# Hybrid decoder layer on one core: constants in three packed arrays, their transpositions and the bias product right behind the first tile's, one cast given to VectorE

## The chip, the cores and the metric

The kernel runs on 1 core of one Trainium2 chip. The metric is the device time of one execution in microseconds (us), lower is better. Before the change it was measured in three runs.

## What is computed

One decoder layer over 512 tokens of 1024 features, all in float32. Cut to what matters here:

```python
u = rms_norm(x, norm_mix_g)
proj = u @ w_in                       # q 1024, k 256, v 256, conv value and gate 2048, two gates 2048
q = rms_norm(q, q_norm_g) * HEAD_DIM ** -0.5
k = rms_norm(k, k_norm_g)
attn = sliding_window_attention(q, k, v, attn_sinks, rel_bias) @ w_attn_o   # window 128, bias by distance bucket
h = a * sigmoid(gate)
h = depthwise_conv(h, w_dw) + b_dw    # 31 taps, 1024 channels
conv = silu(layer_norm(h, conv_ln_g, conv_ln_b)) @ w_conv_out
x = x + (sigmoid(gate_attn) * attn + sigmoid(gate_conv) * conv) @ w_out
x = x + square(relu(rms_norm(x, norm_mlp_g) @ w_ff1)) @ w_ff2
```

The constants that the change speaks of are small: `w_dw` (31 rows of 1024), `b_dw`, `conv_ln_g` and `conv_ln_b` (one row of 1024 each), `rel_bias` (32 x 16), a one-hot array of 32 x 128 that maps distances to buckets, `q_norm_g` and `k_norm_g` (64 each) and `attn_sinks` (16).

## The kernel before

Every operand of a product is split into a high part (rounded to fp32r) and a low part (the remainder), and a product is three matmuls: high by high, low by high, high by low. So weights arrive as `raw_...` tiles, ScalarE casts the high half, and GpSimd or VectorE subtracts to get the low half.

*Start.* The 512 tokens are four tiles of 128. For each tile ScalarE squares and sums (`x_square`, L296), VectorE finishes the root and scales (`x_scale`, L300, output `u`), TensorE transposes (L207, eight transpositions into `tp_u`), ScalarE casts the high part out of PSUM (`uTh`, L209) and VectorE the remainder (`uTl`, L210). The key weights `raw_k` come in two halves of 512 rows; `hi_lo` (L305) casts one half (L307) and returns the function that subtracts (L308). `k_proj` (ps_k, L316, L317 and, with the low weights, L320) and `v_proj` (ps_v, the same lines) follow for each tile. Before the first tile's transpositions TensorE runs `WARM` = 20 matmuls of the identity with itself into a PSUM tile that nobody reads, and between these transpositions and the first `k_proj` it runs `FILL` = 4 more of them (a float32 matmul is two passes, so the profile has 40 and 8).

*Constants.* All loads of this time go through SP's queue. The constants come in nine loads behind the x tiles and the k and v weights: `gq`, `gk`, the sinks, `w_dw`, `b_dw`, `conv_ln_g`, `conv_ln_b`, `rel_bias`, `oh`. The four that hold channels land in one tile `rows` of 34 partitions. `columns` (L358) transposes it on TensorE in eight pieces into `wc_ps`, multiplies `rel_bias` by the one-hot array into `rel_ps`, and on VectorE copies both out (`wcol`, `lnh`, `rel`); `rel` goes to DRAM, from where the attention bias is read back. `columns` is the first of the events that follow the k and v projections.

*Order.* The start is written out by hand (the block under `manual_schedule`, from L1367) for TensorE, VectorE, ScalarE and GpSimd; each engine takes its instructions in that order. After the last `v_proj` the list `events` is sorted by position and called: at -2 the constants, at 0 the first tile of the convolution's gate (`ps_g`, L498 to L500), at 0.4 `k_norm`, at 4.5 the cast of the normed keys (`k2h`, L397), at 9.5 their transposition (`ktp_h`, L405).

*SP's loads.* A load counts up one of eight completion counters, which are taken in turn. SP issues in order, and a load that takes a counter again waits until the load before it on that counter has landed in full. So the ninth load on SP waits for the landing of the first, the tenth for that of the second, and so on, if nothing else holds it longer. Before, the order is: x tile 0, gmix, raw_k (two halves), x tile 1, raw_v (two halves), x tiles 2 and 3, and the nine constants. A later load of weights also waits until its buffer (`raw`, two buffers) is free.

Of the kernel before, what the change touches and what calls it, by code (L numbers as in the profile page):

```python
# [17 lines left out]
P = 128  # L18
# [21 lines left out]
RATES = ((16, 1.0), (42, 1.9), (152, 1.35), (1e9, 1.8))  # L40
WARM = 20
FILL = 4
EARLY = 3
# [10 lines left out]
def tile_hybrid_block(  # L54
# [4 lines left out]
    w_in: bass.AP,  # L59
    q_norm_g: bass.AP,  # L60
    k_norm_g: bass.AP,
    attn_sinks: bass.AP,
    rel_bias: bass.AP,
    w_attn_o: bass.AP,
    w_dw: bass.AP,
    b_dw: bass.AP,
    conv_ln_g: bass.AP,
    conv_ln_b: bass.AP,
    w_conv_out: bass.AP,
# [3 lines left out]
    w_ff2: bass.AP,  # L73
    onehot: bass.AP,
    out: bass.AP,
# [150 lines left out]

    warm_up(WARM)

    def load_x(t):
# [19 lines left out]

    rows = att.tile([P, D], F32, name="rows", tag="qraw", bufs=2)  # L250
    rb_sink = whole_lines(keep, P, LINE // 4, "rb_sink")
    rb = rb_sink[0:32, 16:16 + NQ]
    oh = sm.tile([32, P], F32, name="oh", tag="osb", bufs=1)
    gq = keep.tile([P, HD], F32, name="gq")
    gk = keep.tile([P, HD], F32, name="gk")
    nsink = rb_sink[:, 32:32 + NQ]
    nc.sync.dma_start(gq, bc(q_norm_g[0], P))
    nc.sync.dma_start(gk, bc(k_norm_g[0], P))
    nc.sync.dma_start(nsink, bc(attn_sinks[0], P))
    nc.sync.dma_start(rows[0:CW, :], w_dw[0])  # L260
    nc.sync.dma_start(rows[CW:CW + 1, :], b_dw)
    nc.sync.dma_start(rows[CW + 1:CW + 2, :], conv_ln_g)
    nc.sync.dma_start(rows[CW + 2:CW + 3, :], conv_ln_b)
    nc.sync.dma_start(rb, rel_bias)
    nc.sync.dma_start(oh, onehot)

# [90 lines left out]

    def columns():  # L358
        wc_ps = ps1.tile([P, KD, NR], F32, name="wc_ps", tag="s")
        for k in range(KD):  # L360
            pe.transpose(wc_ps[:, k, :], rows[0:NR, k * P:(k + 1) * P], ident[0:NR, 0:NR])
        rel_ps = ps1.tile([P, P], F32, name="rel_ps", tag="s")
        pe.matmul(rel_ps[0:NQ, :], rb, oh, start=True, stop=True)
        ve.memset(rel, NEG)
        ve.tensor_copy(wcol, wc_ps)
        ve.tensor_scalar(out=wcol[:, :, 0:CW], in0=wc_ps[:, :, 0:CW], scalar1=0.5, scalar2=None, op0=ALU.mult)
        ve.tensor_scalar(out=lnh, in0=wc_ps[:, :, CW + 1:CW + 3], scalar1=0.5, scalar2=None, op0=ALU.mult)
        ve.tensor_copy(rel[:, P:2 * P], rel_ps[0:NQ, :])
        nc.sync.dma_start(rel_d, rel)

    def rep(ap, n):
# [36 lines left out]

    at(-2, columns)
    at(0.4, k_norm)  # L410
# [955 lines left out]

    with tc.manual_schedule(engines=START_ENGINES):  # L1367
        se.activation(roots[:, 0:1], epsc, AF.Sqrt)
        x_square(0, ss0)
        x_scale(0, rsqrt_root(root[0], mean_eps(ss0, D, 1, "x0"), 1, "x0"))  # L1370
        lo0 = hi_lo(kw, kw_raw, 0, se.copy, ge)
        lo0()
        load(0)
        x_trans(0)
        warm_up(FILL)
        lo1 = hi_lo(kw, kw_raw, 1, se.copy, ve)
        lo1()
# [36 lines left out]
        ksum()
        for _ in vp:
            pass
        k_proj(3)()
        for _ in v_proj(3):
            pass
        for _, _, fn, args in sorted(events, key=lambda e: e[:2]):  # L1420
            fn(*args)


_INS = ["x", "norm_mix_g", "w_in", "q_norm_g", "k_norm_g", "attn_sinks", "rel_bias", "w_attn_o", "w_dw", "b_dw",
        "conv_ln_g", "conv_ln_b", "w_conv_out", "w_out", "norm_mlp_g", "w_ff1", "w_ff2"]
_OUT = (S, D)
# [33 lines left out]
```

## Time and profile before

| what | value |
|---|---|
| median of 3 runs | 758.69 us (757.81 to 758.85) |
| the profiled execution's own time | 757.91 us |
| its span, first to last instruction | 756.1 us |
| granted TensorE clock, mean | 0.999 |
| TensorE (PE) busy | 750.6 us, 99% |
| VectorE (DVE) busy | 606.0 us, 80% |
| ScalarE (ACT) busy | 441.3 us, 58% |
| GpSimd (POOL) busy | 273.4 us, 36% |

Times in the profile are microseconds from the first instruction. PE is TensorE's matmuls, PEld its weight loads, SPq the issue of a load by SP. "out<-in" names the tile written and the tiles read, L and a number is a line of the kernel before. A bracket at a row's end says how long the engine had been idle and what ended it. The chain is followed back from the last instruction to what released it. A windows row gives a stretch, its length, the busy time of each engine with the number of starts in parentheses, the granted clock (1.00 is full), the share of the 16 DMA engines and GB/s. A DMA row gives 40 equal slices of its stretch.

### The profile page before, as it was taken

The page shows a single profiled execution, that of the slowest core. Times are in us where ns is not written, and L with a number is a line of the kernel's source. Part 1 is how long each engine was busy: PE and PEld are TensorE (multiplying, and loading weights), DVE is VectorE, ACT ScalarE, POOL GpSimd, SP SyncE. Part 2 cuts the span into 40 slices and gives each one's busy share as a digit, 9 for nine tenths or more (in the row PEclk, how much of TensorE's full clock was granted, in tenths as well). Part 3 has the DMA queues.
Part 4 walks back from the last instruction along what each step waited for, and adds up shares of the span by engine and source line. Part 5 has one row for each costly group of instructions (what it writes and reads, how often), then busy time and mean ns, then how long its engine had stood idle before and what let it go on. Part 6 is the DMA issues. An engine that isn't in the chain of part 4 may idle for free.

```text
span 756.1 us, 11678 instructions
## 1 busy us (share of the span) xinstructions
PE 750.6 (99%) x4474; PEld 663.6 (88%) x4474; DVE 606.0 (80%) x928; ACT 441.3 (58%) x697; POOL 273.4 (36%) x214
## 2 busy tenths in 40 slices
PE   9999999999999999999999999999999999999997
PEld 8989989898888888888888899988998899889986
DVE  5466998789878988878346679899879987998795
ACT  7445457757666665339235357864676467636861
POOL 1453968948774566443531002210121012101210
PEclk9999999999999999999999999999999999999999
DMA  7441040312314113531338205983498349834772
GB/s 262 149 161 56 1 168 15 126 56 81 115 61 137 56 55 112 168 111 56 112 111 294 97 29 91 263 198 117 127 230 200 112 123 228 203 116 115 171 162 111
DMA packets 66014, 97.48 MB, mean 129 GB/s; under 512 B 3540, under 2 KB 36612, under 8 KB 65958
## 3 DMA queue, kind: packets, MB, share of 16 engines
q1 hardware_dynamic: 56710, 78.91, 31.2%
q0 software_dynamic: 9248, 17.83, 13.4%
q8 instruction: 35, 0.57, 0.3%
q14 instruction: 21, 0.17, 0.1%
HBM read 94.60 MB, written 2.12 MB: 128 GB/s over the span
## 4 chain that ended last, share of the span: by engine, by line
PE 98%; DVE 2%; issue 0%; POOL 0%; DVEq 0%; POOLq 0%
PE ps_x L1177 12%; PE ps_z L1182 12%; PE ps_y L1182 6%; PE ps_y L1177 6%; PE ps_z L1177 3%; PE ps_x L1182 3%; PE ps_g L498 2%; PE ps_q L197 2%; PE ps_q L198 2%; PE ps_q L199 2%; PE ps_a L498 2%; PE ps_ta L498 2%; PE ps_a L500 2%; PE ps_g L500 2%; PE ps_g L499 2%; PE ps_ta L500 2%
## 5 line engine op out<-in xcount | busy, mean ns | idle before, releaser
L1148 DVE TENSOR_TENSOR piecel<-block,pieceh 128x1024 fp32r<-128x1024 f32 x112 | 135.7, 1219 | 27.8 <-ACT pieceh L1145 27.6
L1145 ACT CAST pieceh<-block 128x1024 fp32r<-128x1024 f32 x112 | 116.7, 1050 | 67.5 <-DVE block L1138 21.7
L803 DVE SCALAR_TENSOR_TENSOR cv<-h,wcol,cv 128x512 f32<-128x512 f32 x208 | 146.2, 746 | 0.5
L1124 POOL DMA_DIRECT2D block<-in_w_ff_dram x34 | 41.3, 1241 | 287.3 <-DVE piecel L1148 157.1
L1177 PE MATMUL ps_x<-xSh,pieceh 128*128 128x256 f32 x192 | 53.0, 276 | 0.0
L1177 PE MATMUL ps_x<-xSl,pieceh 128*128 128x256 f32 x192 | 53.0, 276 | 0.0
L1177 PE MATMUL ps_x<-xSh,piecel 128*128 128x256 f32 x192 | 53.0, 276 | 0.0
L711 ACT ACTIVATE s<-s,negm 128x257 f32<-128x257 f32 (+1 forms) x64 | 30.4, 479 | 16.0 <-DVE negm L703 16.0
L1182 PE MATMUL ps_z<-piecel,aSh 128*128 128x512 f32 (+1 forms) x98 | 37.9, 387 | 0.0
L1182 PE MATMUL ps_z<-pieceh,aSh 128*128 128x512 f32 (+1 forms) x98 | 37.7, 385 | 0.0
L1182 PE MATMUL ps_z<-pieceh,aSl 128*128 128x512 f32 (+1 forms) x98 | 37.7, 385 | 0.0
L1138 DVE TENSOR_TENSOR block<-block,block 128x1024 f32<-128x1024 f32 x30 | 36.5, 1221 | 0.8 <-DMA block<-in_w_ff_dram 0.4
L795 POOL TENSOR_TENSOR side<-side,tap 128x512 f32<-128x512 f32 x24 | 31.2, 1298 | 15.1 <-ACT tap L794 15.1
L197 PE MATMUL ps_q<-wh_q,uTh 128*128 128x256 f32 x128 | 36.5, 285 | 0.0
L199 PE MATMUL ps_q<-wh_q,uTl 128*128 128x256 f32 x128 | 36.2, 283 | 0.0
L198 PE MATMUL ps_q<-wl_q,uTh 128*128 128x256 f32 x128 | 36.2, 283 | 0.0
L1177 PEld LDWEIGHTS ps_x<-xSh,piecel 128*128 128x128 f32 x192 | 36.0, 188 | 0.0
L1177 PEld LDWEIGHTS ps_x<-xSh,pieceh 128*128 128x128 f32 x192 | 36.0, 188 | 0.0
L1177 PEld LDWEIGHTS ps_x<-xSl,pieceh 128*128 128x128 f32 x192 | 36.0, 188 | 0.0
L735 DVE TENSOR_TENSOR pTl<-ptp,pTh 128x512 fp32r<-128x512 f32 x28 | 19.0, 686 | 17.8 <-ACT pTh L731 17.8
L720 POOL TENSOR_TENSOR s<-s,r 128x1024 f32<-128x1024 f32 (+1 forms) x16 | 26.9, 1684 | 16.7 <-DVE r L715 16.7
L1216 ACT CAST aSh<-c 128x1024 fp32r<-128x1024 f32 x16 | 16.8, 1053 | 21.4 <-DVE c L1230 11.7
(325 smaller groups left out, 2531.8 us busy)
## 6 DMA issues: line engine op xcount, KB each, us to landing
block<-in_w_ff_dram SPq DMA_DIRECT2D x64, 512.0 KB, 5.5
block<-in_w_ff_dram POOLq DMA_DIRECT2D x34, 512.0 KB, 6.9
x<-in_x_dram SPq DMA_DIRECT2D x8, 512.0 KB, 4.2
raw_g<-in_w_in_dram SPq DMA_DIRECT2D x8, 512.0 KB, 4.4
raw_a<-in_w_in_dram SPq DMA_DIRECT2D x8, 512.0 KB, 3.5
raw_q<-in_w_in_dram SPq DMA_DIRECT2D x8, 512.0 KB, 4.5
raw_ta<-in_w_in_dram SPq DMA_DIRECT2D x8, 512.0 KB, 4.3
raw_tc<-in_w_in_dram SPq DMA_DIRECT2D x8, 512.0 KB, 3.5
```

What stands on the lines that cost most here:

```text
L197: pe.matmul(ps, ah, wh, start=first, stop=False)
L198: pe.matmul(ps, ah, wl, start=False, stop=False)
L199: pe.matmul(ps, al, wh, start=False, stop=last)
L498: pe.matmul(ps, wh[:, k, :], ah(k), start=(k == 0), stop=False)
L500: pe.matmul(ps, wl[:, k, :], ah(k), start=False, stop=(k == KD - 1))
L803: ve.scalar_tensor_tensor(out=cps[ct], in0=src, scalar=w, in1=cps[ct], op0=ALU.mult, op1=ALU.add)
L1124: ge.dma_start(tl["raw"][buf][:, ks, :], block(ph, i, j)[:, ks, :], accum_op=ALU.add)
L1138: ve.tensor_tensor(out=o, in0=a, in1=b, op=ALU.add)
L1145: se.copy(piece("h", n), tl["raw"][buf][:, 2 * h:2 * h + 2, :])
L1148: ve.tensor_tensor(out=piece("l", n), in0=tl["raw"][buf][:, 2 * h:2 * h + 2, :], in1=piece("h", n).bitcast(F32), op=ALU.subtract)
L1177: pe.matmul(o, b[:, c, w], a[:, k, :], start=(first and c + q + i == 0), stop=(k == 3 and i == 2), skip_group_check=True)
L1182: pe.matmul(acc[:, cols], a[:, k, w], b[:, c, cols], start=(first and c + i == 0), stop=(k == 3 and i == 2), skip_group_check=True)
```

## The change

Three packed arrays, joined before the launch, take the place of nine: `vectors` (q_norm_g, k_norm_g, attn_sinks: 144 numbers), `buckets` (rel_bias and the one-hot array: 32 x 144) and `channels` (w_dw, b_dw, conv_ln_g, conv_ln_b: 34 x 1024). `channels` and `buckets` are loaded right behind raw_k, ahead of x tile 1; `vectors` behind x tile 3. `columns` is cut in two: `columns_in` (TensorE) takes the place of the four filler matmuls, and `columns_out` (VectorE and the write of `rel`) stays where `columns` was. Both results of `columns_in` share one PSUM bank. `WARM` is 17 instead of 20 and stands in the block that is written by hand. The high cast of raw_k's first half goes from ScalarE to VectorE.

```diff
-WARM = 20
-FILL = 4
+WARM = 17
...
-    warm_up(WARM)
...
     nc.sync.dma_start(gmix, bc(norm_mix_g[0], P))
+    rows = att.tile([P, D], F32, name="rows", tag="qraw", bufs=2)
+    bucket = sm.tile([32, NQ + P], F32, name="bucket", tag="osb", bufs=1)
+    rb, oh = bucket[:, 0:NQ], bucket[:, NQ:NQ + P]
     load_kv(kw_raw, Q_END, 0)
     load_kv(kw_raw, Q_END, 1)
+    nc.sync.dma_start(rows[0:CW + 3, :], channels)
+    nc.sync.dma_start(bucket, buckets)
     xt.append(load_x(1))
...
-    nc.sync.dma_start(gq, bc(q_norm_g[0], P))
-    nc.sync.dma_start(gk, bc(k_norm_g[0], P))
-    nc.sync.dma_start(nsink, bc(attn_sinks[0], P))
-    nc.sync.dma_start(rows[0:CW, :], w_dw[0])
-    nc.sync.dma_start(rows[CW:CW + 1, :], b_dw)
-    nc.sync.dma_start(rows[CW + 1:CW + 2, :], conv_ln_g)
-    nc.sync.dma_start(rows[CW + 2:CW + 3, :], conv_ln_b)
-    nc.sync.dma_start(rb, rel_bias)
-    nc.sync.dma_start(oh, onehot)
+    vecs = whole_lines(keep, P, 3 * LINE // 4, "vecs")
+    gq, gk, nsink = vecs[:, 0:HD], vecs[:, HD:2 * HD], vecs[:, 2 * HD:2 * HD + NQ]
+    nc.sync.dma_start(vecs[:, 0:2 * HD + NQ], bc(vectors[0], P))
...
-    def columns():
-        wc_ps = ps1.tile([P, KD, NR], F32, name="wc_ps", tag="s")
+    def columns_in():
+        bank = ps1.tile([P, S], F32, name="wc_rel", tag="s")
+        wc_ps = bank[:, 0:KD * NR].rearrange("p (k n) -> p k n", n=NR)
         for k in range(KD):
             pe.transpose(wc_ps[:, k, :], rows[0:NR, k * P:(k + 1) * P], ident[0:NR, 0:NR])
-        rel_ps = ps1.tile([P, P], F32, name="rel_ps", tag="s")
+        rel_ps = bank[:, S - P:S]
         pe.matmul(rel_ps[0:NQ, :], rb, oh, start=True, stop=True)
+        cols_ps.extend((wc_ps, rel_ps))
+
+    def columns_out():
...
+    at(-2, columns_out)
...
-    at(-2, columns)
...
     with tc.manual_schedule(engines=START_ENGINES):
+        warm_up(WARM)
...
-        lo0 = hi_lo(kw, kw_raw, 0, se.copy, ge)
+        lo0 = hi_lo(kw, kw_raw, 0, ve.tensor_copy, ge)
         lo0()
         load(0)
         x_trans(0)
-        warm_up(FILL)
+        columns_in()
```

TensorE at its start, before and after (`wc_rel` is the shared PSUM bank, `bucket` holds both operands of the bias product; the line numbers after are smaller by 7 to 17 here):

```order
L225 MATMUL warm<-ident 128x128 x20
L207 MATMUL tp_u_0_183<-ident,u_167 128x128 x4
L207 MATMUL tp_u_1_190<-ident,u_167 128x128 x4
L225 MATMUL warm<-ident 128x128 x4
L316 MATMUL ps_k_208<-kw_152,uTh 128x256
L317 MATMUL ps_k_208<-kw_152,uTl 128x256
```

```order
L218 MATMUL warm<-ident 128x128 x17
L200 MATMUL tp_u_0_172<-ident,u_156 128x128 x4
L200 MATMUL tp_u_1_179<-ident,u_156 128x128 x4
L347 MATMUL wc_rel<-ident,rows 128x34 x8
L349 MATMUL wc_rel<-bucket 16x128
L299 MATMUL ps_k_203<-kw_124,uTh 128x256
L300 MATMUL ps_k_203<-kw_124,uTl 128x256
```

The filler between the transpositions and the first `k_proj` became nine instructions that wait for two loads. Those loads, in SP's queue before and after:

```order
L231 DMA x_115<-in_x_dram 128x1024
L241 DMA gmix<-in_norm_mix_g_dram 128x1024
L235 DMA raw_k<-in_w_in_dram 128x4x256 x2
L231 DMA x_122<-in_x_dram 128x1024
L235 DMA raw_v<-in_w_in_dram 128x4x256 x2
L231 DMA x_127<-in_x_dram 128x1024
L231 DMA x_129<-in_x_dram 128x1024
L257 DMA gq<-in_q_norm_g_dram 128x64
L258 DMA gk<-in_k_norm_g_dram 128x64
L259 DMA rb_sink<-in_attn_sinks_dram 128x16
L260 DMA rows<-in_w_dw_dram 31x1024
```

```order
L222 DMA x_95<-in_x_dram 128x1024
L232 DMA gmix<-in_norm_mix_g_dram 128x1024
L226 DMA raw_k<-in_w_in_dram 128x4x256 x2
L238 DMA rows<-in_channels_dram 34x1024
L239 DMA bucket<-in_buckets_dram 32x144
L222 DMA x_106<-in_x_dram 128x1024
L226 DMA raw_v<-in_w_in_dram 128x4x256 x2
L222 DMA x_111<-in_x_dram 128x1024
L222 DMA x_113<-in_x_dram 128x1024
L248 DMA vecs<-in_vectors_dram 128x144
L441 DMA raw_g_169<-in_w_in_dram 128x4x256 x2
```

The constants' 34 rows moved from behind x tile 3 to ahead of x tile 1 and raw_v. TensorE again, at the end of the last `v_proj`, before and after:

```order
L320 MATMUL ps_v_487<-vw_155,uTh 128x256 x8
L361 MATMUL wc_ps<-ident,rows 128x34 x8
L363 MATMUL rel_ps<-oh,rb_sink 16x128
L498 MATMUL ps_g_534<-uTh,wh_g_0_364 128x512
L499 MATMUL ps_g_534<-uTl,wh_g_0_364 128x512
```

```order
L303 MATMUL ps_v_482<-vw_127,uTh 128x256 x8
L490 MATMUL ps_g_518<-uTh,wh_g_0_359 128x512
L491 MATMUL ps_g_518<-uTl,wh_g_0_359 128x512
L492 MATMUL ps_g_518<-uTh,wl_g_0_360 128x512
L490 MATMUL ps_g_518<-uTh,wh_g_0_359 128x512
```

The first gate tile now follows the v projection directly. On ScalarE the cast of raw_k's first half is gone ahead of the first `uTh`, and on VectorE it stands between `x_scale` of tile 0 and the first `uTl`; nothing else moves on these two engines.

More of the change, by code (lines that the diff above doesn't have):

```diff
@@ L59, in tile_hybrid_block @@
     w_in: bass.AP,
[L60 to L63, printed above, removed]
+    vectors: bass.AP,
+    buckets: bass.AP,
     w_attn_o: bass.AP,
[L65 to L68, printed above, removed]
+    channels: bass.AP,
     w_conv_out: bass.AP,
@@ L73, in tile_hybrid_block @@
     w_ff2: bass.AP,
-    onehot: bass.AP,
     out: bass.AP,
@@ L248, in tile_hybrid_block @@
     xt += [load_x(2), load_x(3)]
[L250 to L256, printed above, removed]
-    nc.sync.dma_start(gq, bc(q_norm_g[0], P))
-    nc.sync.dma_start(gk, bc(k_norm_g[0], P))
[L259 to L262, printed above, removed]
-    nc.sync.dma_start(rows[CW + 2:CW + 3, :], conv_ln_b)
-    nc.sync.dma_start(rb, rel_bias)
-    nc.sync.dma_start(oh, onehot)
+    vecs = whole_lines(keep, P, 3 * LINE // 4, "vecs")
+    gq, gk, nsink = vecs[:, 0:HD], vecs[:, HD:2 * HD], vecs[:, 2 * HD:2 * HD + NQ]
+    nc.sync.dma_start(vecs[:, 0:2 * HD + NQ], bc(vectors[0], P))
     uTh = keep.tile([P, KD, S], F32R, name="uTh", tag="act", bufs=2)
@@ L356, in tile_hybrid_block @@
     rel_d = dr.tile([NQ, 3 * P], F32, name="rel_d")
-    def columns():
-        wc_ps = ps1.tile([P, KD, NR], F32, name="wc_ps", tag="s")
+    cols_ps = []
+    def columns_in():
+        bank = ps1.tile([P, S], F32, name="wc_rel", tag="s")
+        wc_ps = bank[:, 0:KD * NR].rearrange("p (k n) -> p k n", n=NR)
         for k in range(KD):
             pe.transpose(wc_ps[:, k, :], rows[0:NR, k * P:(k + 1) * P], ident[0:NR, 0:NR])
-        rel_ps = ps1.tile([P, P], F32, name="rel_ps", tag="s")
+        rel_ps = bank[:, S - P:S]
         pe.matmul(rel_ps[0:NQ, :], rb, oh, start=True, stop=True)
+        cols_ps.extend((wc_ps, rel_ps))
+    def columns_out():
+        wc_ps, rel_ps = cols_ps
         ve.memset(rel, NEG)
@@ L1421, in tile_hybrid_block @@
             fn(*args)
-_INS = ["x", "norm_mix_g", "w_in", "q_norm_g", "k_norm_g", "attn_sinks", "rel_bias", "w_attn_o", "w_dw", "b_dw",
-        "conv_ln_g", "conv_ln_b", "w_conv_out", "w_out", "norm_mlp_g", "w_ff1", "w_ff2"]
+_INS = ["x", "norm_mix_g", "w_in", "vectors", "buckets", "w_attn_o", "channels", "w_conv_out", "w_out", "norm_mlp_g",
+        "w_ff1", "w_ff2"]
 _OUT = (S, D)
@@ L1449 @@
     nc = _bacc.Bacc("TRN2", target_bir_lowering=False, num_devices=1, dynamic_dma_scratch_size=2048)
+    packed = dict(inputs)
+    packed["vectors"] = _np.concatenate([inputs[n] for n in ("q_norm_g", "k_norm_g", "attn_sinks")], axis=1)
+    packed["buckets"] = _np.concatenate([inputs["rel_bias"], _bucket_onehot()], axis=1)
+    packed["channels"] = _np.concatenate([inputs["w_dw"][0]] + [inputs[n] for n in ("b_dw", "conv_ln_g", "conv_ln_b")])
     arrays, args = {}, []
-    for name in _INS + ["onehot"]:
-        a = _bucket_onehot() if name == "onehot" else _np.ascontiguousarray(inputs[name])
+    for name in _INS:
+        a = _np.ascontiguousarray(packed[name])
         arrays[f"in_{name}_dram"] = a
```

## The prediction

> **What bounds the kernel now.** I read the page first, then TensorE's waits, the chain of the first 18 us and of 34 to 40 us, then the loads of that time. From the page (busy time; the chain's shares by engine), and from the waits of TensorE:
>
> ```profile
> PE 750.6 (99%) x4474; PEld 663.6 (88%) x4474; DVE 606.0 (80%) x928; ACT 441.3 (58%) x697; POOL 273.4 (36%) x214
> ...
> PE 98%; DVE 2%; issue 0%; POOL 0%; DVEq 0%; POOLq 0%
> ...
> PE warm L225 <- POOL eps_ln L122: 1.5, 1, 1.5
> ```
>
> TensorE is the bound from start to end, and the only wait listed for it is the first 1.5 us. So a microsecond that TensorE loses or saves near the start reaches the end, and work on the other engines counts only where TensorE waits for it. The chain (start, length, what), first at the start, then at the end of the k and v projections:
>
> ```profile
> 1.47 7.24 PE warm L225 x40
> 8.71 0.87 PE tp_u L207 x8
> 9.59 0.89 PE warm L225 x8
> 10.48 0.12 PE ps_k L316
> 10.60 0.34 PE ps_k L317
> 10.94 0.11 PE ps_k L316
> ...
> 12.60 0.96 PE ps_k L320 x8
> ...
> 13.57 0.39 PE ps_v L316
> ...
> 14.79 0.21 PE ps_v L316
> ...
> 37.17 0.61 PE wc_ps L361 x8
> 37.78 0.32 PE rel_ps L363 x2
> ```
>
> The warm-up matmuls are filler, but they stand on the chain: the first transpositions start behind them at 8.71 although their input is ready at 7.85 (row L300 below: 6.57 + 1.28). The eight matmuls at 9.59 are filler as well; the k projection runs steadily from its third matmul, 10.94. The eight transpositions of the constants and the bias product at 37.17 hold TensorE for 0.61 + 0.32 = 0.93 us. ScalarE and VectorE at the start (timeline: start, busy):
>
> ```profile
> 6.57 1.28 DVE L300 SCALAR_TENSOR_TENSOR u<-x,roots,gmix 128x1024 f32<-128x1024 f32 x1 [0.34 <-DMA gmix<-in_norm_mix_g_dram]
> 7.86 1.04 ACT L307 CAST kw<-raw_k 128x1024 fp32r<-128x1024 f32 x1 [2.40 <-DMA raw_k<-in_w_in_dram]
> 9.19 1.07 ACT L209 CAST uTh<-tp_u 128x512 fp32r<-128x512 f32 x2 [0.28 <-PE tp_u L207]
> 11.10 1.07 ACT L296 ACTIVATE u<-x 128x1024 f32<-128x1024 f32 x1
> 12.49 2.06 ACT L307 CAST vw<-raw_v 128x1024 fp32r<-128x1024 f32 x2
> 11.24 1.23 DVE L308 TENSOR_TENSOR kw<-raw_k,kw 128x1024 fp32r<-128x1024 f32 x1
> ```
>
> **When the loads land.** SP's issue times tell it, because from the ninth load on SP waits for the landing of the load eight places ahead: L259 for raw_k's second half, L260 for x tile 1, L261 and L262 for the halves of raw_v, L264 for x tile 3, the second L449 for the 31 rows of w_dw.
>
> ```profile
> 9.59 0.33 SPq L259 DMA_DIRECT2D rb_sink<-in_attn_sinks_dram  x1
> 10.81 0.30 SPq L260 DMA_DIRECT2D rows<-in_w_dw_dram  x1
> 12.14 0.23 SPq L261 DMA_DIRECT2D rows<-in_b_dw_dram  x1
> 13.50 0.22 SPq L262 DMA_DIRECT2D rows<-in_conv_ln_g_dram  x1
> 16.04 0.32 SPq L264 DMA_DIRECT2D rb_sink<-in_rel_bias_dram  x1
> 20.61 0.92 SPq L449 DMA_DIRECT2D raw_a<-in_w_in_dram  x2
> ...
> SPq L449 <- DMA rows<-in_w_dw_dram: 1.9, 1, 1.9
> ```
>
> x tile 1, 128 rows of 4 KB, lands 10.81 - 9.59 = 1.22 us behind raw_k's second half: 8 rows on each of 16 DMA engines, 0.153 us per row. The 31 rows of w_dw, less than a quarter of it, land only at 20.61, 4.6 us behind x tile 3. The DMA view of 16.1 to 17.5 us (40 slices of 0.035 us) shows why:
>
> ```profile
> DMA  0200020002000020002000020104100020002000
> GB/s 0 117 0 0 0 117 0 0 0 117 0 0 0 0 117 0 0 0 117 0 0 0 0 117 7 13 6 127 13 2 2 0 117 0 0 4 117 0 0 0
> ```
>
> One row of 4 KB (117 GB/s in 0.035 us) goes at a time, nine from slot 2 to slot 37, again 0.153 us apart: one DMA engine carries them all, 31 x 0.153 = 4.74 us. Equal shares explain both loads: 128 rows divide into 16 shares, 31 into no equal shares but one. This is the row that decides my forecast, because the packed array that TensorE now waits for at the start has 34 rows, which divide into two shares of 17.
>
> [...]
>
> **The change, part by part.**
>
> *Warm-up, 20 to 17.* Six passes of the last, fast kind go, 7.24 us / 40 at most 0.18 each: up to 1.1 us, of which 8.71 - 7.85 = 0.86 can be used. The transpositions end at 8.7 to 8.9 instead of 9.59.
>
> *FILL out, the constants in.* Their 34 rows queue behind raw_k's second half. The engine with the 31 rows of w_dw began them at 20.61 - 4.74 = 15.87, though x tile 3 and three small loads stood ahead of them and x tile 3 landed on the slowest engine at 16.04: it runs at least 0.2 us ahead of the slowest, with some 0.2 for each small load about 0.7. So raw_k's half is through there at 8.9 and the constants at 8.9 + 17 x 0.153 = 11.5 (bounds: 16 shares, three rows each, 9.4; one share of 34, 14.1). I take two shares. TensorE then stands from about 8.9 to 11.5, spends 0.93 on the constants (the bucket array lands meanwhile), and reaches the third matmul of the k projection at 12.67 instead of 10.94: +1.73. Its 24 matmuls end at 15.3 instead of 13.55.
>
> *What queues behind the 34 rows.* x tile 1 and raw_v lose 2.6 us on the same two engines, plus about 0.2 for the bucket array: x tile 1 at 10.81 - 0.7 + 2.8 = 12.9, raw_v at 14.2 and 15.6. ScalarE does things in order: the square of tile 1 moves from 11.10 to 12.9, the first raw_v cast to 14.3, done 15.35 (TensorE arrives at 15.3); the second cast is done at 15.6 + 1.03 = 16.65, and the fifth k step of the v projection (14.79 before) starts at about 16.8. TensorE is now 2.0 us late. x tile 2 lands near 16.9, and its square moves from 15.0 to 17.0; x tile 3 has more room.
>
> *37.17 us.* The constants' 0.93 us go there: +2.0 - 0.93 = +1.07.
>
> *VectorE's cast* lies from 7.86 to about 9.1 (priced like L308, 1.23, though that reads two inputs; ScalarE's own takes 1.04). It is hidden: the next VectorE work feeds the k projection, which waits for the constants until 12.4. With that cover gone it could cost some 0.3. GpSimd's remainder then runs 9.1 to 11.5, needed from 14.3: nothing.
>
> *columns_out* stays on VectorE, 0.93 us later against TensorE. It ends in the cast below, and the user starts 4.5 us behind that cast's end: nothing.
>
> ```profile
> 45.25 1.99 ACT L397 CAST k2h<-kraw 128x1024 fp32r<-128x1024 f32 x2
> 51.78 0.46 PE L405 MATMUL ktp_h<-ident_r,k2h 128*128 128x128 f32 x4
> ```
>
> *SP.* Six loads fewer, and raw_g and raw_a issue earlier. TensorE waits for neither today, so nothing.
>
> *The clock.* TensorE now idles for 2.6 us. The windows view (stretch, length, busy of PE (starts), PEld, DVE, ACT, POOL, granted clock, DMA):
>
> ```profile
> 3.35:6.76 3.41, 3.41 (x18) 3.41 (x17) 0.99 (x6) 1.44 (x3) 0.00 (x0) 1.00 0.93 259
> 6.76:8.00 1.24, 1.24 (x13) 1.24 (x13) 1.09 (x1) 0.14 (x1) 0.00 (x0) 1.00 1.08 377
> 750.87:754.28 3.41, 1.36 (x12) 1.16 (x10) 1.41 (x3) 0.00 (x0) 0.00 (x0) 1.00 0.37 138
> 753.90:754.20 0.30, 0.00 (x0) 0.00 (x0) 0.00 (x0) 0.00 (x0) 0.00 (x0) 1.00 0.59 205
> 754.30:754.60 0.30, 0.00 (x0) 0.00 (x0) 0.00 (x0) 0.00 (x0) 0.00 (x0) 0.50 0.48 161
> ```
>
> At the start the matmuls ran at half pace until 6.76 (18 in 3.41 us, then 13 in 1.24). At the end the clock fell to 0.50 at 754.28, only 2.05 us after the last matmul (750.87 + 1.36). A gap of 2.6 us may thus halve the pace. The price lies between 0 and 2.3: half pace for as long as at the start, 6.76 - 1.47 = 5.3 us, loses 2.65, of which about 0.4 is hidden by the wait for raw_v. I take 0.5, about half of the executions at half that price. [...]
>
> **The sum.** The profiled execution took 757.91 us (its span 756.1 and 1.8 around it), 0.8 below the median of the runs, 758.69. 757.91 + 2.0 - 0.93 + 0.5 = 759.5 us, 0.1% above that median.
>
> **Rivals.**
> *The clock never falls*, because a gap of 2.6 us is too short: the term is 0 and the time 759.0. [...]
> *The clock falls for several microseconds* in most executions: the term is 1.2 to 2.3 and the time 760.2 to 761.3. For it speaks the fall at the end; against it that raw_v's wait hides part.
> *One engine carries all 34 rows*, as it does 31: constants at 14.1, 2.6 us more, with the clock 762. Equal shares of two speak against it.
> *Faster: the rows spread over many engines* and land by 9.4 to 10.0, slowest engine included. Then the warm-up saves 0.3 to 0.6 and 37.17 saves 0.93: 756.4 to 756.7. It decides where the constants land before about 10.3. Against it stands the load of 31 rows, on one engine.
> *No change in effect*: the two engines run further ahead of the slowest than I think, or the v loads hide more: 757.9 to 758.7.
>
> **Chances.** A measurement of this kernel can tell about 0.2%, 1.5 us, from no change: 757.2 to 760.2 counts as the same. Two shares with the clock down in some executions, a term up to 1.1 (759.2 to 760.1): 0.30; two shares and the clock never down (759.0): 0.20; no change in effect: 0.12; long slow clock: 0.20; one engine: 0.08; many engines: 0.10. Slower takes the long slow clock, the one engine and 0.02 of the first case, 0.30; faster the many engines, 0.10; the same 0.60. The range 757.9 to 761.3 leaves out one engine and many engines.
>
> **What would show it.** In the trace after: the first wc_rel transposition near 11.5, with TensorE's wait put down to the load of rows; the square of tile 1 near 12.9 put down to x; the second part of the v projection near 16.8; ps_g following the v projection at 39.2 instead of 38.1; k projection starts 0.21 to 0.23 us apart if the clock fell, 0.12 if not. I am wrong if the constants land before 10.3 or after 13.

## The result, and the profile after

The changed kernel takes 763.32 us (median of 4 runs, 762.79 to 763.83) against 758.77 us for the kernel before on the same chip (757.81 to 758.86): ratio 1.0063, 95% interval 1.0045 to 1.0080: 0.6% slower, and the interval leaves out no change. The forecast was 759.5, range 757.9 to 761.3. The profiled execution is the one of 762.79, 4.9 us above the profiled execution of before.

From the page and from TensorE's waits (total, times, longest):

```profile
PE 750.9 (99%) x4460; PEld 663.6 (87%) x4460; DVE 606.6 (80%) x929; ACT 440.3 (58%) x696; POOL 273.2 (36%) x214
...
PE 89%; DVE 5%; DMA 2%; issue 1%; ACT 1%; SPq 0%; POOL 0%; DVEq 0%; POOLq 0%; ACTq 0%
...
PE wc_rel L347 <- DMA rows<-in_channels_dram: 4.0, 1, 4.0
PE warm L218 <- POOL eps_ln L115: 1.5, 1, 1.5
PE ps_z L1174 <- DVE piecel L1140: 0.4, 1, 0.4
PE ps_x L1169 <- DVE xSl L1212: 0.3, 1, 0.3
```

TensorE's work is the same (750.9 for 750.6), yet three waits are new: 4.0 us for the rows of constants, and two small ones in the MLP, 450 us away from anything that was edited. Of the chain, 11% is no longer TensorE's, where it was 2%. The chain at the start (start, length, what), then ScalarE and VectorE:

```profile
2.67 10.51 DMA rows<-in_channels_dram
13.18 0.04 issue
13.23 0.68 PE wc_rel L347 x8
13.91 0.32 PE wc_rel L349 x2
14.22 0.51 PE ps_k L299
14.73 0.21 PE ps_k L300
14.95 0.21 PE ps_k L299
...
17.50 0.21 PE ps_k L299
17.72 0.12 PE ps_k L300
17.84 0.95 PE ps_k L303 x8
18.80 0.12 PE ps_v L299
```
```profile
7.94 0.69 DVE L290 CAST kw<-raw_k 128x1024 fp32r<-128x1024 f32 x1
14.31 1.06 ACT L279 ACTIVATE u<-x 128x1024 f32<-128x1024 f32 x1 [3.49 <-DMA x<-in_x_dram]
15.69 1.03 ACT L290 CAST vw<-raw_v 128x1024 fp32r<-128x1024 f32 x1
16.87 1.05 ACT L290 CAST vw<-raw_v 128x1024 fp32r<-128x1024 f32 x1 [0.15 <-DMA raw_v<-in_w_in_dram]
```

The 34 rows land at 13.18, not 11.5; the k projection's third matmul is at 14.95 (10.94 before); from 14.2 to 17.6 its matmuls stand 0.21 apart instead of 0.12; and x tile 1 and raw_v are late too, though the v projection then runs without a stop from 18.80. What the engines and the clock did in steps of 3.41 us (stretch, length, busy of PE, PEld, DVE, ACT, POOL with starts, granted clock, DMA share, GB/s):

```profile
7.37:10.78 3.41, 1.83 (x17) 1.59 (x15) 2.55 (x4) 1.98 (x3) 2.06 (x1) 1.00 1.07 358
10.78:14.20 3.42, 0.97 (x11) 0.72 (x11) 1.31 (x1) 0.04 (x1) 0.30 (x1) 1.00 1.09 330
14.20:17.61 3.41, 3.41 (x17) 3.41 (x17) 1.81 (x6) 3.12 (x5) 0.00 (x0) 0.50 1.05 396
17.61:21.02 3.41, 3.41 (x31) 3.41 (x31) 2.54 (x3) 2.30 (x6) 0.00 (x0) 1.00 0.54 191
```

The clock was halved from 14.20 to 17.61, one step, in which TensorE started 17 matmuls instead of about 31.

To see where each microsecond stays, I set TensorE's matmuls beside those of the kernel before, one by one (start after minus start before, us; one profiled execution of each kernel). The experiments stand in the same table:

| kernel | passes | first ps_k | last ps_k of tile 0 | in the v projection | ps_g, 41 us | MLP, 460 us | 500 us | last |
|---|---|---|---|---|---|---|---|---|
| the change | 4460 | +3.9 | +5.2 | +4.8 | +3.7 | +3.6 | +5.0 | +5.0 |
| e1_pad48 | 4460 | +1.5 | +1.3 | +0.9 | -0.1 | -0.1 | +1.0 | +1.0 |
| e2_late_cols | 4460 | -1.0 | -0.6 | +5.7 | +5.6 | +5.5 | +6.0 | +6.0 |
| e3_filled | 4492 | +4.2 | +4.0 | +3.6 | +2.5 | +2.6 | +2.6 | +2.6 |
| e4_late_loads | 4460 | -0.8 | -0.4 | -0.3 | -0.2 | -0.2 | +0.6 | +0.6 |
| e5_pad48_fill | 4474 | +1.5 | +1.3 | +0.9 | 0.0 | 0.0 | 0.0 | 0.0 |
| e6_less_warm | 4460 | -0.7 | -0.2 | +0.1 | +0.2 | +0.1 | +1.4 | +1.9 |
| e7_late_warm | 4474 | +0.2 | +0.2 | +0.2 | +0.1 | +0.1 | 0.0 | 0.0 |
| e9_pad128 | 4460 | +1.6 | +2.6 | +2.4 | +1.3 | +1.3 | +2.4 | +2.4 |
| e12_transposed | 4474 | +0.7 | +0.5 | +0.1 | -0.5 | -0.5 | -0.4 | -0.4 |
| e14_pad35 | 4460 | +1.1 | +2.3 | +1.9 | +0.9 | +0.9 | +2.0 | +2.0 |

So the 5.0 us are three losses less two gains: about 3.9 lost by the first matmul of the k projection, 1.3 while the clock is halved, and 1.4 between 460 and 500 us; 1.1 gained between the v projection and ps_g (the 0.93 us of the constants, gone from there), and 0.5 in small steps on the way.

### The profile page after: what moved, and what is told of

Same layout as the page of the kernel before. It is cut to its first block, busy times and chain, and to the rows that moved or that the text cites. A ratio compares the mean times of both kernels' runs of the same rounds, so it can differ in the third digit from the quotient of the medians.

```text
span 761.0 us, 11641 instructions
## 1 busy us (share of the span) xinstructions
PE 750.9 (99%) x4460; PEld 663.6 (87%) x4460; DVE 606.6 (80%) x929; ACT 440.3 (58%) x696; POOL 273.2 (36%) x214
## 4 chain that ended last, share of the span: by engine, by line
PE 89%; DVE 5%; DMA 2%; issue 1%; ACT 1%; SPq 0%; POOL 0%; DVEq 0%; POOLq 0%; ACTq 0%
PE ps_z L1174 11%; PE ps_x L1169 10%; PE ps_y L1174 5%; PE ps_y L1169 4%; PE ps_x L1174 3%; PE ps_z L1169 2%; PE ps_q L190 2%; PE ps_g L490 2%; PE ps_q L192 2%; PE ps_q L191 2%; PE ps_a L490 2%; PE ps_ta L490 2%; PE ps_a L492 2%; PE ps_g L492 2%; PE ps_g L491 2%; PE ps_ta L492 2%
```

## The experiments

Times before are 758.08 us (e1 to e4), 758.13 (e5 to e8 and e9 to e12) and 757.81 (e13, e14; a single run), each on the same chip as the kernels compared with it.

### The rows on more engines, the gap filled, the constants elsewhere

**e1_pad48.** The changed kernel with 14 rows of zeros behind the 34:

```diff
-    nc.sync.dma_start(rows[0:CW + 3, :], channels)
+    nc.sync.dma_start(rows[0:48, :], channels)      # channels has 48 rows
```

> The channels array is padded to 48 rows, so that 16 DMA engines carry three rows each; nothing else is changed from the changed kernel. Theory A (the 34 rows go on two engines, 17 each, and TensorE, x tile 1 and raw_v queue behind them): the rows land at 9.6 to 10.0 us instead of 13.2, TensorE waits under 1.2 us, the clock does not fall, the square of x tile 1 starts near 11.0 instead of 14.3; time 756.5 to 757.8. Rival R (every transfer at that place is slow, 255 GB/s instead of 390 in the profile after, whatever the shares): the rows land at 10.5 to 11.5 and the time is 758.5 to 759.5.

Measured: 759.70 us (10 runs), ratio 1.0019 (1.0010 to 1.0029). The rows land at 10.71, where the rival had them and not theory A, and TensorE waits for them 1.7 us instead of 4.0. So spreading the rows brings most of the wait back, but they do not run at the pace of theory A (see "Why the rows were slow"). The ten times fall into two groups: five executions with a mean granted clock of 1.00 take 758.68 to 759.30, five with 0.997 or 0.998 take 760.10 to 760.90. A mean of 0.997 or 0.998 is what one step of 3.41 us at half clock gave in e9, e14 and the changed kernel, so the gap of 1.7 us halved the clock in five of ten executions, and that cost some 1.4 us. The five at full clock are still 0.6 to 1.2 us above the kernel before; in the profiled one of them that is the loss in the MLP (table).

**e2_late_cols.** The changed loads, but the constants transposed at their old place:

```diff
+    at(-2, columns_in)
...
-        columns_in()
```

> The loads are those of the changed kernel, but the transpositions of the constants and the bias product go back to the place ahead of the first gate tile, without filler. Theory A: TensorE no longer waits for the 34 rows, but x tile 1 and raw_v still queue behind them on two engines, so the square of tile 1 still starts near 14.3 and the v projection near 16.7 instead of 13.6; time 761 to 762.5. Rival (the wait of TensorE alone is the loss): 757 to 758.

Measured: 763.85 us (4 runs), ratio 1.0077 (1.0062 to 1.0092), no better than the change. TensorE no longer waits for the rows, it waits behind them:

```profile
PE ps_v L299 <- ACT vw L290: 3.9, 1, 3.9
```

x tile 1 and raw_v are as late as the rows, and ScalarE, in order behind the square of x tile 1, casts raw_v as late. Either wait alone, 3.9 us here and 4.0 in the changed kernel, costs nearly the same; they are not added. The time is above the 761 to 762.5 of theory A because the clock falls here too, for two steps (columns as in the windows above):

```profile
12.40:15.81 3.41, 0.57 (x5) 0.36 (x4) 0.15 (x1) 1.40 (x4) 0.00 (x0) 1.00 1.06 402
15.81:19.22 3.41, 2.38 (x11) 2.38 (x12) 3.19 (x7) 3.25 (x6) 0.00 (x0) 0.50 0.98 348
```

From the first to the last matmul of the v projection the delay grows from 3.3 to 5.6 us.

**e3_filled.** The changed kernel with 16 filler matmuls ahead of the constants, to keep the clock up:

```diff
         x_trans(0)
+        warm_up(16)
         columns_in()
```

> The changed kernel with 16 filler matmuls ahead of the constants' transpositions, so that TensorE is busy while it waits. The load still lands near 13.2. Theory A with the clock as a term of its own: the clock does not fall, the k projection runs at 0.12 us per matmul, and the time is 1.2 to 1.9 below the changed kernel, 761.3 to 762.1. Rival (the slow clock is hidden behind the late raw_v): 763.0 to 763.6.

Measured: 760.23 us (8 runs), ratio 1.0026 (1.0015 to 1.0037), and the clock stays at 1.00 in all eight. The rows are as late as ever (landing at 13.46), the k projection as late, but it runs at full pace, and nothing is lost in the MLP. That the time lies below the 761.3 to 762.1 of theory A comes with this second point, which the theory did not have. The medians put 763.32 - 760.23 = 3.1 us on the two together, the profiled executions 5.0 - 2.6 = 2.4.

**e4_late_loads.** The packed arrays loaded behind x tile 3, the constants transposed at their old place; WARM 17, no FILL and VectorE's cast stay:

```diff
-    nc.sync.dma_start(rows[0:CW + 3, :], channels)
-    nc.sync.dma_start(bucket, buckets)
...
     xt += [load_x(2), load_x(3)]
+    nc.sync.dma_start(rows[0:CW + 3, :], channels)
+    nc.sync.dma_start(bucket, buckets)
...
+    at(-2, columns_in)
...
-        columns_in()
```

> The packed arrays are loaded behind x tile 3, as the nine arrays were, and the constants are transposed ahead of the first gate tile; what stays of the change is WARM 17, no filler after the transpositions, and VectorE's cast. Theory A: nothing of the loss is left, and the shorter warm-up gives 0.3 to 0.7 us: 757.0 to 758.2. Rival (VectorE's cast or the moved loads of later weights cost something): 759 or more.

Measured: 758.68 us (10 runs), ratio 1.0009 (0.9999 to 1.0018): the whole loss at the start comes with the place of the load. The time is 0.5 us above the range that I had expected. In the profile 0.8 us are lost at 460 to 500 us, as in the changed kernel. Nothing that I edited lies there.

### The loss in the MLP

The rows that show it: before, the stretch of 465 to 472 us has one packet of the queue that loads instructions (16 KB in the trace, 0.02 MB in the view), 0.8% of 16 engines x 7 us, which is 0.9 us; after, the packet of the same place takes 2.1%, 2.4 us. A load of w_ff that is under way beside it lands late, and ScalarE's cast waits for that (before, then after):

```profile
q8 instruction: 1, 0.02, 0.8%
...
470.59 1.05 ACT L1145 CAST pieceh<-block 128x1024 fp32r<-128x1024 f32 x1 [0.49 <-DMA block<-in_w_ff_dram]
```
```profile
q8 instruction: 1, 0.02, 2.1%
...
468.23 7.42 DMA block<-in_w_ff_dram
...
475.72 1.05 ACT L1137 CAST pieceh<-block 128x1024 fp32r<-128x1024 f32 x1 [1.97 <-DMA block<-in_w_ff_dram]
```

My theory: TensorE runs 14 passes fewer (4460 for 4474), so the place in its instructions where the next 16 KB are fetched comes later against the rest, just when GpSimd's loads of w_ff are under way. Two runs take the number of passes alone.

**e6_less_warm.** The kernel before with 14 passes fewer and nothing else:

```diff
-WARM = 20
-FILL = 4
+WARM = 17
+FILL = 0
```

> The kernel before with WARM 17 and FILL 0 and nothing else changed: 14 passes of TensorE fewer, all loads, casts and transpositions of the constants as before. Theory of the instruction fetch: the 16 KB packet near 466 us comes later against TensorE's work, meets the loads of w_ff on GpSimd's queue, takes 1.5 us or more instead of 0.95, and TensorE loses 0.6 to 1.3 us between 465 and 500 us, with the wait of ps_z on piecel listed; start 0.2 us earlier to 0.1 later: 758.3 to 759.2 in the profile, 0.3 to 1.1 above the kernel before. Rival (the loss comes of the packed arrays' start, by a shift in time or by other addresses): packet at 0.95 us, no wait of ps_z, 757.6 to 758.1.

Measured: profiled at 759.78 us, with the loss and the wait that the theory names, and the cast late by nearly the same amount:

```profile
PE ps_z L1182 <- DVE piecel L1148: 0.4, 1, 0.4
...
q8 instruction: 1, 0.02, 2.0%
...
472.11 1.05 ACT L1145 CAST pieceh<-block 128x1024 fp32r<-128x1024 f32 x1 [1.87 <-DMA block<-in_w_ff_dram]
```

GpSimd issues that load at the same point of TensorE's work as before (464.73 for 464.58, TensorE 0.15 late), but it lands after 7.30 us, where before the cast could start some 6.0 us behind the issue. The packet starts at 466.67 instead of 465.77, 0.8 us later against TensorE. So it is the load's time to land that is longer, and it goes with the passes alone; that the packet holds the load up, and that not something third slows both, is argued. How the passes set the packet's place is open too: with 18 passes more than before (e3) it starts at 468.40, only 0.1 us later against TensorE.

The median of e6's 11 runs is 758.65, ratio 1.0007 (0.9999 to 1.0016), so the price differs from execution to execution and the profiled one was the dearest.

**e7_late_warm.** e4 with WARM 20 and the four FILL matmuls put back, 4474 passes:

> The packed arrays loaded behind x tile 3, VectorE's cast kept, the constants transposed at the old place, and now WARM 20 and FILL 4 as before, so that TensorE has its old 4474 passes: the packing and the cast alone. Theory of the instruction fetch: the 0.6 us that the same kernel with WARM 17 and no FILL lost near 468 us are gone, no ps_z wait on piecel; the start is within 0.1 us of the kernel before; 757.8 to 758.2. Rival (the packed arrays cause the loss): 758.4 to 758.9 with that wait.

Measured: 758.46 us (11 runs), ratio 1.0001 (0.9992 to 1.0010). The packet takes 0.9%, TensorE has no wait but the first, and it is level with the kernel before to the end. In this execution the packing and the cast alone change nothing; the median, though, lies in the range of the rival, whose wait the trace does not show.

Over all profiled executions the rule has no exception: the ten kernels with 4460 passes have that packet at 1.6 to 2.4 us and lose 0.5 to 1.8 us behind 460 us; the five other variants, with 4474 or 4492, have it at 0.95 to 0.96 us and lose nothing there. In the times it is worth less where it is alone: e6 and e4 stand 0.5 and 0.6 us above before, e7 0.3, and the intervals of the three overlap. So it is the traces that show this loss; the times of these three runs cannot tell it from none.

### Why the rows were slow

I had priced a row at 0.153 us. In the profile after, the stretch of 10.5 to 12.5 us shows the packets of the other loads slowed as well as the rows (those of 1 KB take 0.067 us in the mean for 0.046; before first, then after):

```profile
DMA packets 757, 0.79 MB, mean 395 GB/s; under 512 B 25, under 2 KB 744, under 8 KB 757
```
```profile
DMA packets 493, 0.53 MB, mean 267 GB/s; under 512 B 18, under 2 KB 477, under 8 KB 493
```

After, 16 packets of 4 KB in 2.0 us (493 - 477), each 0.25 us long in the mean by the trace, so two in flight at a time: two engines at 0.25 us per row. The engine count of my forecast holds, the pace doesn't. The place of the load is not the reason for this pace: in e4, behind x tile 3, the same 34 rows run no faster. Nor is it simply that other loads move beside them: in the kernel before, the last of w_dw's 31 rows went beside the loads of raw_g and kept their pace (e4 from 17 to 18 us, then before from 19.4 to 20.2):

```profile
DMA packets 230, 0.26 MB, mean 257 GB/s; under 512 B 3, under 2 KB 222, under 8 KB 230
```
```profile
DMA packets 261, 0.28 MB, mean 349 GB/s; under 512 B 3, under 2 KB 256, under 8 KB 261
```

Eight packets of 4 KB in 1.0 us by two engines are 0.25 us per row, with all of them at 257 GB/s; five in 0.8 us by one engine are 0.16, at 349. Five variants of the load look for the cause.

**e8_pitch**: rows 4352 bytes apart in memory. **e9_pad128**: padded to 128 rows. **e10_spread**: written to every third partition. **e13_one_engine**: loaded as 31 and 3 rows. **e14_pad35**: one row of padding.

```diff
+    nc.sync.dma_start(rows[0:CW + 3, :], channels[:, 0:D])                      # e8, channels 34 x 1088
+    nc.sync.dma_start(rows, channels)                                           # e9, channels 128 x 1024
+    nc.gpsimd.memset(rows, 0.0)                                                 # e10
+    nc.sync.dma_start(rows[0:100:3, :], channels)
+    nc.sync.dma_start(rows[0:CW, :], channels[0:CW, :])                         # e13
+    nc.sync.dma_start(rows[CW:CW + 3, :], channels[CW:CW + 3, :])
+    nc.sync.dma_start(rows[0:35, :], channels)                                  # e14, channels 35 x 1024
```

> The changed kernel, with the 34 rows of the constants 4352 bytes apart in memory instead of 4096 (64 unused columns behind each row). Theory A (the two DMA engines read from addresses that collide in memory, and slow everything beside them): a row's packet takes 0.16 to 0.18 us again, the rows land at 11.5 to 12.0 as I had forecast, TensorE's wait for them is 2.4 to 2.8 us instead of 4.0, and the time is 760.5 to 762. Theory B (the collision is on the receiving side, at the 34 partitions, or in the engines): nothing changes, rows at 13.2, packets of 0.25 us, 762.5 to 764.

> The changed kernel with the 34 rows of the constants padded to 128: 16 DMA engines, eight rows each, over all 128 partitions, 2.7 times the data of the 48 rows. With 34 rows on 34 partitions and with 48 rows on 48 partitions every packet in flight took 1.5 to 2 times as long. Theory A (the slow pace comes from writing to few of the 128 partitions): no packet is slowed, 4 KB in 0.16 us, the rows land 8 x 0.153 = 1.2 us behind raw_k, at 10.5 to 10.9, no later than the 48 rows, and TensorE stands 1.5 to 1.9 us for them. Theory B (the slow pace goes with a load of constants at this place, wherever it is written): 4 KB packets of 0.25 to 0.33 us, rows at 11.6 or later, TensorE's wait 2.5 us or more.

> The changed kernel with its 34 rows written to every third partition (0, 3, ... 99) instead of partitions 0 to 33, still by two DMA engines, 17 rows each. TensorE transposes partitions 0 to 33 as before, so the constants in the output are not the reference's: only the load's pace is read. Theory A (few partitions on the receiving side): the packets of a row take 0.16 to 0.20 us, the rows land at 11.6 to 12.2, TensorE's wait falls from 4.0 to 2.5 to 3.1 us. Theory B (the two engines themselves, or the reading side): 0.25 us per row, rows at 13.0 or later, wait 3.8 us or more.

> The changed kernel with its 34 rows loaded as 31 and 3, which one DMA engine carries, at the same place, partitions 0 to 33. In the kernel before, one engine carried 31 rows at 0.155 us each beside the loads of raw_g and slowed nobody. Theory A (two engines beside each other cause the slow pace): packets of 4 KB at 0.16, of 1 KB at 0.046 us, the last row lands at 9.3 + 34 x 0.155 = 14.6, and TensorE stands 5.3 to 5.8 us. Theory B (few partitions are the cause, whoever writes): 1 KB packets at 0.06 us or more, rows at 0.2 us or more, landing behind 16.0, TensorE's wait 6.8 us or more. The clock falls in either case; 765 to 769 us.

> The changed kernel with a single row of padding, 35 rows: seven DMA engines carry five rows each, on partitions 0 to 34. Theory A (few partitions: eight of them together take in 4 KB per 0.153 us, however many engines write, which is what the 48 rows showed, six groups of eight in 1.2 us): the first four groups of eight take 8 x 0.153 = 1.2 us, so the packets take about 0.24 us and the rows land at 10.4 to 10.9; TensorE stands 1.5 to 1.9 us. Theory B (the number of engines alone matters, and seven are enough): 0.16 us per packet, 5 x 0.155 = 0.8 us, rows at 9.9 to 10.3, TensorE stands 1.0 to 1.4 us. In both 758.3 to 760.9 us, by whether the clock falls.

The chain's row of the load in each (issue, time to landing), in the order e8, e9, e10, e13 (its last load), e14, and then e1:

```profile
2.68 10.57 DMA rows<-in_channels_dram
```
```profile
2.67 8.15 DMA rows<-in_channels_dram
```
```profile
3.77 10.09 DMA rows<-in_channels_dram
```
```profile
3.15 12.87 DMA rows<-in_channels_dram
```
```profile
2.67 7.68 DMA rows<-in_channels_dram
```
```profile
2.66 8.05 DMA rows<-in_channels_dram
```

| load | engines x rows | landed, us | time of the run, us |
|---|---|---|---|
| the change | 2 x 17 | 13.18 | 762.79 |
| e8, other pitch in memory | 2 x 17 | 13.25 | 764.26 |
| e10, every third partition | 2 x 17 | 13.86 | 764.30 |
| e13, 31 and 3 rows | 1 x 31, 3 x 1 | 16.02 | 765.92 |
| e14, 35 rows | 7 x 5 | 10.35 | 759.76 |
| e1, 48 rows | 16 x 3 | 10.71 | 759.70 (median) |
| e9, 128 rows | 16 x 8 | 10.82 | 760.18 |

(The engines are my estimate by equal shares, as in the prediction, from the 128 rows of x tile 1, whose 4 KB packets go some 16 at a time in the trace of before, and the 31 of w_dw, one at a time. By these the last 3 rows of e13 go on three engines, not on the one that I had named; one engine carries 31. In e8, e10 and e13 the clock fell for two steps, in the profiled executions of the change, e9 and e14 for one, so the times differ by more than the landings.) Another pitch in memory leaves landing and pace as they were, 272 GB/s for 267 from 10.5 to 12.5 us: theory A of e8 falls. With 128 rows no 4 KB packet is slowed, all take 0.159 us, as theory A of e9 says: 48 rows on 48 partitions take as long as 128 rows on all (landed at 10.71 and 10.82). The DMA view of 9.5 to 10.5 us, e1 and then e9:

```profile
DMA packets 70, 0.23 MB, mean 226 GB/s; under 512 B 8, under 2 KB 16, under 8 KB 70
```
```profile
DMA packets 160, 0.42 MB, mean 416 GB/s; under 512 B 31, under 2 KB 63, under 8 KB 160
```

So for many engines the pace went with the number of partitions, in one profiled execution of each: 226 GB/s with the rows on 48 of them, 416 with the rows on 128. What it is in the partitions that sets the pace, no run shows; the groups of eight in theory A of e14 were my estimate from the 48 rows. e14 landed at 10.35, ahead of the two others and between the ranges of its two theories, so it does not decide between them.

For two engines it is not settled. e10 differs in more than the partitions: the memset holds its rows back, and SP issues them behind x tile 1 (3.77) instead of ahead of it (2.67). So its landing tells less than its pace: 0.20 to 0.23 us per row against 0.25, between the two theories. With one engine (e13) most other packets keep their 0.046 us, as theory A says, but the rows land at 16.02, as theory B says, since the engine's own packets take up to 0.36 us in places. So two engines with 34 rows slowed the loads beside them at both places, one engine did so less (342 GB/s in e13 from 10.5 to 12.5 us), and it was slow itself in e13 but not in the kernel before. Why is open.

### The clock

The windows of e9, of e1 and of e14 at their gaps (columns as above):

```profile
9.62:13.03 3.41, 2.16 (x20) 1.91 (x21) 2.47 (x3) 1.91 (x3) 1.53 (x1) 1.00 1.05 394
13.03:16.45 3.42, 3.42 (x18) 3.42 (x18) 2.81 (x7) 2.64 (x6) 0.00 (x0) 0.50 1.05 409
```
```profile
7.11:10.52 3.41, 1.97 (x18) 1.73 (x16) 2.66 (x4) 1.82 (x3) 1.75 (x1) 1.00 1.09 330
10.52:13.93 3.41, 3.18 (x28) 2.93 (x29) 2.01 (x6) 2.28 (x5) 0.60 (x1) 1.00 1.06 386
```
```profile
8.90:12.32 3.42, 1.99 (x19) 1.67 (x19) 2.71 (x3) 2.54 (x4) 2.05 (x1) 1.00 1.05 362
12.32:15.73 3.41, 3.41 (x18) 3.41 (x18) 2.78 (x7) 2.57 (x5) 0.00 (x0) 0.50 1.06 412
```

In every trace here the clock changes only at steps of 3.413 us from where it first rose: after, 7.37, then 14.20, 17.61 and at the end 761.72, which is 221 steps on; before, 6.76 and 754.28, which is 219 steps. The first rise lies between 4.86 and 7.37 us, so the steps fall elsewhere in each execution. e1's gap of 1.68 us lies across a step (10.52), is shared by two windows, and the clock stays. e9's gap of 1.84 us and e14's of 1.43 (8.96 to 10.40) share their window with the short matmuls of the constants, and the clock falls for one step. It fell after windows in which TensorE was listed as busy for 0.97 (the change), 1.99 (e14) and 2.16 (e9) of 3.41 us.

The listed busy time alone does not decide it: e1's window with 1.97 kept the clock, e14's with 1.99 lost it. The last windows of the executions, in which no constants are transposed, are cleaner. The two that lie closest are e4's, at whose end (754.69) the clock fell, and e5's, at whose end (754.08) it stayed:

```profile
751.27:754.69 3.42, 1.52 (x13) 1.32 (x11) 1.44 (x3) 0.00 (x0) 0.00 (x0) 1.00 0.32 120
750.67:754.08 3.41, 1.59 (x13) 1.38 (x11) 1.44 (x3) 0.00 (x0) 0.00 (x0) 1.00 0.31 115
```

Over all the traces no window that began at full clock kept it with 1.52 us or less, and of those with 1.59 or more only e9's and e14's lost it. In these two the short matmuls of the constants make up about 1 us of the listed time (0.68 + 0.32 in the chain of each). So they seem to count for less than is listed; no run takes them alone.

### Versions without the loss

**e5_pad48_fill.** e1 with seven filler matmuls ahead of the constants:

```diff
         x_trans(0)
+        warm_up(7)
         columns_in()
```

> The rows padded to 48, so that 16 DMA engines carry them, and seven filler matmuls (14 passes, 14 x 0.11 = 1.55 us) between the first tile's transpositions and the constants', where TensorE otherwise stands for 1.7 us. TensorE has then as many instructions as before (4474 passes). Theory (the clock falls in a gap of 1.7 us in part of the executions, and 14 passes fewer move an instruction fetch into the way of the MLP's weight loads): the clock stays at 1.00 in every execution, TensorE stands less than 0.4 us for the rows, is at most 0.2 us ahead of or behind the kernel before at the raw_g projection (ps_g), loses nothing near 465 us, no ps_z wait on piecel is listed, and the time is 757.4 to 758.3, no higher than before. Rival on the clock (it falls through something else at the start): some executions still at 760 to 761. Rival on the second loss (the packed arrays or the other start cause it): 0.9 us behind again from 470 us on, 758.7 to 759.3.

Measured: 757.78 us (11 runs), ratio 0.9995 (0.9986 to 1.0004); clock 1.00 but for one execution at 0.999, wait for the rows 0.2 us, nothing lost in the MLP:

```profile
PE 750.4 (99%) x4474; PEld 663.4 (88%) x4474; DVE 606.9 (80%) x929; ACT 440.4 (58%) x696; POOL 273.2 (36%) x214
...
PE wc_rel L347 <- DMA rows<-in_channels_dram: 0.2, 1, 0.2
```

That is all of the change's loss, removed by 14 rows of zeros and 14 passes of filler. It is not a gain: by the v projection the start has cost 0.9 us (table), and that is saved near 37 us.

**e11_act_cast.** e5 with the first half of the key weights cast by ScalarE again:

```diff
-        lo0 = hi_lo(kw, kw_raw, 0, ve.tensor_copy, ge)
+        lo0 = hi_lo(kw, kw_raw, 0, se.copy, ge)
```

> The padded and filled kernel with the first half of the key weights cast by ScalarE, as in the kernel before, instead of VectorE. My pricing says that the cast lies beside other work on either engine: the k projection starts within 0.15 us of the kernel with VectorE's cast (its first matmul at 11.76), the v projection too, and the span is within 0.3 us of 756.0. Rival: ScalarE's copy of the transposed tile comes later behind the cast, and the k projection starts 0.3 to 1.0 us later, 757 in the span.

Measured: 757.33 us (one run), and the k projection starts within 0.02 us of e5's. The cast costs nothing on either engine. The 0.4 us by which the span is shorter arise later than 300 us, in a single execution.

**e12_transposed.** The constants packed in transposed order (128 rows of 272 numbers), so that TensorE has none of them to transpose; late loads as in e7, from which it differs so:

```diff
-        for k in range(KD):
-            pe.transpose(wc_ps[:, k, :], rows[0:NR, k * P:(k + 1) * P], ident[0:NR, 0:NR])
...
-        warm_up(4)
+        warm_up(2)
+        for _ in range(6):
+            pe.matmul(warm[:, 0:16], ident, ident[:, 0:16], start=True, stop=True)
```

> The constants packed in transposed order, 128 rows of 34 x 8 values, loaded behind x tile 3, so that TensorE need not transpose them at all; the bias product stays at its old place. WARM 20, FILL 2 and six short filler matmuls keep TensorE at 4474 passes, where the instruction fetch did no harm. By my theory (TensorE's stream sets the time, and the second loss comes from the fetch alone): nothing at the start beyond 0.2 us, 0.61 us gained near 37.2, kept to the end, no ps_z wait on piecel: 757.2 to 757.7, 0.4 to 0.6 us below the kernel before, which is less than 0.1% and hardly told apart by the times. Rival (the gain near 37.2 is given back later): ps_g 0.6 us ahead, but the last matmul within 0.2 us of the kernel before; 757.9 to 758.4.

Measured: 757.55 us (11 runs), ratio 0.9993 (0.9984 to 1.0002). TensorE is 0.48 us ahead at ps_g and 0.38 at the end: the 0.61 us are gained and kept, less 0.1 at the start. It is the lowest median of the kernels with several runs, but its interval holds no change.

## Why the prediction was wrong

*FILL out, the constants in*: the step that failed. Two engines were right, 17 x 0.153 us was not. That pace came from 31 rows that one engine carried; with two engines it was 0.25 us per row, and the landing was at 13.18 instead of 11.5 (the start at 8.9 fits: 13.18 - 17 x 0.25 = 8.9). I had set 13 as the bound beyond which I am wrong. That 34 rows make two shares was my estimate from the two loads of before, and the 0.2 us for each small load was a guess that no run takes alone. I priced two engines by a row of one. That hardly anything else moved in the stretch that I read is not the whole reason: the same 31 rows kept their pace later, beside 349 GB/s. What slows two engines is open. Term: +1.73 forecast at the third matmul of the k projection, +4.0 measured (14.95 for 10.94), of which 0.2 are the clock's.

*The clock*: wrong in size: 0.5 taken, 1.3 in the profiled execution for one step of 3.41 us, where the gap was 4.0 us instead of 2.6. The other three executions had a mean clock of 0.994 or 0.995 where the profiled one had 0.998, so about two steps (an estimate from e8, which has two and 0.995). That it may fall within a gap shorter than 3.4 us is right; the changed kernel's gap can't show it, e14's of 1.43 does. The row that I rested it on, the fall 2.05 us behind the last matmul, was read wrongly: it is no delay, 754.28 is the 219th step from 6.76, the end of a window in which TensorE was busy for 1.36 us.

*What queues behind the 34 rows*: the order of events is right (square of x tile 1 at 14.31 put down to x, forecast 12.9), the term is not. I charged TensorE another 0.27 at the fifth k step of the v projection; that step waits for nothing, because the k projection ended at 18.80. e2 shows that this wait by itself is as long as the other, 3.9 for 4.0.

*37.17 us*: right, -0.93 forecast, about -1.1 measured between the v projection and ps_g.

*VectorE's cast*: right that it is hidden (e11); priced at 1.23 after a row with two inputs, it took 0.69.

*columns_out*, *SP*: right, nothing. *Warm-up*: the six passes were priced at 0.18 us, the mean of slow and fast ones; by the windows row (13 in 1.24 us) they are worth 0.57, and the transpositions ended at 9.2, not at 8.7 to 8.9. The wait for the rows hides it.

*What the list did not have*: the loss in the MLP, 1.4 us in the profiled execution. I treated passes that leave the warm-up as time only; by the traces their number also goes with a slow instruction packet 450 us later.

Together: the forecast was +2.0 - 0.93 + 0.5 = +1.57, the profiled execution lost 5.0. The rows are 1.9 of the difference, the loss in the MLP 1.4, the clock 0.8, less 0.7 in the steps that gained.

Of the rivals, the slow clock for several microseconds (760.2 to 761.3) was the right kind, and its term of 1.2 to 2.3 holds the 1.3; its time is too low by the rows and the MLP. Many engines and one engine both fell by the 16 packets above, though the landing came near the 14.1 of one engine by another way.

## What to carry to other kernels

Price a load by one that is cut into the same shares: here two engines with 17 rows each ran at 0.25 us per row in the changed kernel and, at another place, in e4; one engine ran at 0.16 in the kernel before, though not in e13. Look at how many engines and how many partitions it gets: one row of padding (35 for 34) brought the rows 2.8 us earlier, and 128 rows landed with 48 (10.82 and 10.71). Watch gaps in front of TensorE well below the step of 3.41 us: one of 1.43 us cost a step at half clock, and one of 1.7 us did in five of ten executions, about 1.4 us each. Since the place of the steps changes with each execution, a single profile can miss it. When the number of instructions on an engine changes, look for new waits far behind the edit, beside the packets of the instruction queue.

## What had not been expected of the hardware

At 465 to 475 us a 16 KB packet of the instruction queue took 0.95 to 0.96 us in the six kernels with 4474 or 4492 passes and 1.6 to 2.4 in the ten with 4460, and the load beside it was late by 1.4 to 1.5 us in the two of these read above (the change and e6). Other loads beside it do not make it slow by themselves: the next packet of the kernel before (481.86 to 482.78) took 0.92 us while 390 GB/s moved. And two DMA engines with 17 rows of 4 KB each lowered what all sixteen moved together from 395 to 267 GB/s; with the rows on every third partition it was 316, in a run whose loads were also issued in another order. Another pitch in memory did not change it, and its cause is open.
